# One product of the second input phase as seven inner products, its sums loaded by the next block

## The chip, the cores and the metric

The kernel runs on one core of one Trainium2 chip. The metric is the device time of one execution in microseconds, lower is better; where several runs are shown, their median is meant. TensorE multiplies a stationary operand (loaded by its own instruction) by a moving one into PSUM banks; VectorE (DVE), ScalarE (ACT) and GpSimd (POOL) work elementwise; SyncE (SP) issues most DMAs, POOL some.

## The reference

```python
def pool_mixer(h, in_w, group_w, group_b, scale, out_w):
    b, s, _ = h.shape
    u, gate = jnp.split(h @ in_w, 2, axis=-1)
    ug = u.reshape(b, s, POOL_GROUPS, POOL_GROUP_DIM)
    pooled = jnp.stack([trailing_mean(ug[:, :, g], w) for g, w in enumerate(POOL_WINDOWS)],
                       axis=2) - ug
    mixed = jnp.einsum('bsgc,gcd->bsgd', pooled, group_w) + group_b
    y = mixed.reshape(b, s, POOL_WIDTH) * scale * jax.nn.silu(gate)
    return y @ out_w
...
    h = x
    for i in range(DEPTH):
        normed = rms_norm(h, norm_w[i])
...
            h = h + pool_mixer(normed, pool_in_w[j], pool_group_w[j], pool_group_b[j],
                               pool_scale[j], pool_out_w[j])
    return rms_norm(h, final_norm_w)
```

DEPTH is 1, so there is one such layer: 4096 rows of 1024 channels, float32; the input projection has 2048 columns (1024 pooled over trailing windows of 2, 4, 8 and 16 rows in four groups of 256, and 1024 that become the SiLU gate), the output projection 1024.

## The kernel before

**The products.** The group maps are folded into the input weights at the start, so that three phases of dense products are left: `a` (pooled groups 0 and 1 with their gates), `b` (groups 2 and 3 with theirs, the *second input phase*) and `o` (the output projection). Phases `a` and `b` run over 4 blocks of 1024 rows (TB, NB); a block multiplies 1024 channels by 1024 columns as one step of Strassen's method in Winograd's form: seven products P1 to P7 of 512 x 512 x 512 in place of eight, in the order P1, P2, P7, P6, P5, P4, P3 (ORDER_IN, line 32). The list `steps` (line 1069) holds all of them, and the loop at line 1325 writes them out one by one.

**One product.** Every float32 operand is split into a high and a low half (`split`, line 167: ACT copies the high half rounded to float32r, DVE subtracts it from the source), and a product is made of three passes (high x high, high x low, low x high; `mm3`, line 598). `product_in` (line 609) issues 2 halves x 4 column tiles x 2 x 3 = 48 matmuls with a 128x128 stationary tile of weights and 512 moving rows. The operands of the activations lie in four buffers `op0` to `op3`, two to a product, so that the split for the next product can begin when the product before the current one leaves its buffers.

**The sums.** With the four quarters of the activations (11, 12, 21, 22), `form_in` (line 547) forms S3 = 11 - 21, S2 = 22 - S3 and S1 = S2 + 11, and `form_s4` (line 592) S4 = 12 - S2, each as two tiles of 128x1024. In phase `a` they are formed from x, normalized by row; `split_in` (line 576) stores four of them (P1, P2, P7 and P4's operands) to `sd` in DRAM on POOL's queue. Phase `b` loads these four (`load_saved`, line 528) and forms the other three again, for every block. The weights of phase `b` are formed from T3 (`save_t3`, line 289: the difference of two saved weight tiles, stored to `t3d`) and loaded parts (`load_wb`, `form_wb`, `split_wb`).

**Results.** Banks 0 to 3 take P1, P2, P7 and P4, banks 4 to 7 P6, P5 and P3, on top of a copy of P1 (`bank_of`, line 607). `evict_in` (line 806) takes the rows out: P2 the first gate, P6 and P4 the second, P7 and P5 the rows of one half, P3 those of the other. `pool` (line 745) then does the trailing sums on DVE, multiplies with the gate and stores to `yd` on SP's queue; `pool_later` (line 1116) says how many steps later it is written.

**Order.** Each engine's queue is filled by a scheduler that goes by the order of the program text, by when operands are modelled to be ready, by `issue_after` (not ahead of a given instruction on that engine) and by `high_priority`. SBUF tiles come from two lists of slots, 11 of `st` and 8 of `vt`; `take` picks the one that has been free longest, `give` returns it, and a load into a slot waits for the slot's last user. `keep` takes a slot out for good.

**An inner level** is there already in phase `o`: the product P2 of blocks 2 to 7 is done as seven products of half the size (`split_inner`, `product_inner`, `add_inner`, lines 669 to 711) with matmuls of 256 columns (line 701).

Of the kernel before, what the change touches and what calls it, by code (L numbers as in the profile page):

```python
# [35 lines left out]
class Slots:  # L36
# [4 lines left out]
    def __init__(self, tiles):  # L41
        self.free = deque((0, t) for t in tiles)
        self.used = {}

    def age(self):
# [8 lines left out]
    def keep(self):  # L54

        return self.renew(self.free.popleft()[1])

    def give(self, ap):
# [6 lines left out]
def kernel(  # L65
# [53 lines left out]
    st = Slots(sts)  # L119

    def renew(t):
        i = next(i for i, u in enumerate(sts) if u is t)
        return mem.tile([P, D], F32R, tag=f"st{i}", name=f"inner{i}")

    st.renew = renew
    vt = Slots(
# [40 lines left out]
    def split(dst, src):  # L167
# [17 lines left out]
        for i in range(P1, P7 + 1)  # L185
# [3 lines left out]
            i: [dram.tile([P, 2, H], F32, name=f"sd{b}_{i}_{h}") for h in range(2)]  # L189
            for i in (P1, P2, P7, P4)  # L190
        }
# [85 lines left out]
    def load_wb(i):  # L277
        for h in range(2):
# [5 lines left out]
            for name, place, used in (("t3", t3d[h], (P6, P7)), ("22", wvd[2 + h], (P5, P3))):  # L284
                if i in used:
                    p[name] = take()
                    nc.sync.dma_start(out=p[name], in_=place)

    def save_t3():

        for h in range(2):
            us = []
            for k in (h, 2 + h):
                us.append(take())
                nc.sync.dma_start(out=us[-1], in_=wvd[k])
            with tc.issue_after(evicted[0]):
                sub(us[0], us[1], us[0])
            nc.sync.dma_start(out=t3d[h], in_=us[0])
            for u in us:
                give(u)  # L300

# [21 lines left out]
    def split_wb(i):  # L323
        for h in range(2):
            (u,) = parts.pop((i, h)).values()
            if i == P1:
                split_scaled(w[i][h], u, pair(norm_c, h, 0))
            elif i == P2:
                split_scaled(w[i][h], u, pair(norm_c, h, 1))
            else:  # L330
                split(w[i][h], u)
            if i != P6:
                give(u)
# [165 lines left out]
    xs = [{} for _ in range(NB)]  # L499
    turn = [0]  # L500

    def next_op(pattern, **sizes):
# [33 lines left out]
    def load_in(q, b, i):  # L536
        s = xs[b]
        if i == P1:
            s["11"] = load_saved(b, P1) if q else load_x(b, 0, 0)
        elif i == P2:  # L540
            s["12"] = load_saved(b, P2) if q else load_x(b, 0, 1)
        elif i == P7:
            s["21"] = load_saved(b, P7) if q else load_x(b, 1, 0)
        elif i == P6:
            s["22"] = load_saved(b, P4) if q else load_x(b, 1, 1)

    def form_in(q, b, i):

        s = xs[b]
        if i in (P1, P2):  # L550
            if q == 0:
# [24 lines left out]
    def split_in(q, b, i):  # L576
        s = xs[b]
        key = {P1: "11", P2: "12", P6: "2", P7: "21", P5: "11", P4: "22", P3: "12"}[i]
        later = q == 0 and b == 0 and i in (P1, P2)
        t = split_halves(s[key], None if q or later else sd[b].get(i))  # L580
        if later:
            stores.extend(zip(sd[0][i], s[key]))
        if i == P6 and (q or b):
            form_s4(b)
        if i not in (P1, P2, P7, P6):
            for u in s.pop(key):
                give(u)
        return t
# [18 lines left out]
    bank_of = {P1: "x", P2: "x", P6: "y", P5: "y", P3: "y", P7: "v", P4: "v"}  # L607

    def product_in(i, t, sets, by_bank, between=None, behind=None):
        ps = sets[bank_of[i]]  # L610
        halves = [(h, ct) for h in range(2) for ct in range(4)]
# [133 lines left out]
    def pool(b, q, half, vs, sgs):  # L745
# [4 lines left out]
        for g in range(2):  # L750
# [36 lines left out]
            for j in range(2):  # L787
# [3 lines left out]
                )  # L791
            nc.sync.dma_start(
                out=yd[2 * b + 1 - half][:, 2 * grp : 2 * grp + 2, :], in_=sg
# [9 lines left out]
    def cells(us, lo=0):  # L803
        return [us[c // 2][:, c % 2, lo:] for c in range(4)]

    def evict_in(b, q, i, sets, seeds=4):
# [22 lines left out]
        elif i == P4:  # L829
            for c, u in enumerate(cells(ev["21"])):  # L830
                add(halved(u), plain(ps[c]), halved(u))
            for u in ev["21"]:
                copy(u, u, AF.Silu)
        else:
# [269 lines left out]
    def run(n, between=None, behind=None, seeds=4):  # L1104
# [5 lines left out]
        else:  # L1110
            product_in(i, split_up.pop(n), sets, i == P1, between, behind)
            evict_in(b, 0 if kind == "a" else 1, i, sets, seeds)
# [208 lines left out]
    scales, summed = {}, []  # L1321
    stages = (P6, P5, P4)
    stages = (P6, P5, P4)

    for n in range(2, len(steps)):
# [122 lines left out]
```

## Time and profile before

| | |
|---|---|
| time, median of 3 runs | 910.89 us (910.77 to 911.06) |
| the profiled execution: its time, its span | 911.84 us, 909.7 us |
| granted TensorE clock, mean | 0.997 |
| DMA, mean over the span | 196 GB/s |

A line of the chain of waits gives start and length in us, engine and line; one of a group gives line, engine, operation, output<-input, shapes and count, then busy us, mean ns, and the idle time before with what ended it. PE is TensorE's matmul, PEld its weight load; a matmul's duration in the profile includes its pipeline, so that the distance from one to the next is read from the chain. A row of the windows gives the stretch, its length, then busy us and count by engine, the granted clock, the DMA engines' share and GB/s. A line of the timeline gives start, length, engine, line, operation, output<-input and count, and in brackets the idle time before.

### The profile page before, as it was taken

What the parts mean: (1) busy time and instruction counts of PE and PEld (TensorE: products, weight loads), DVE (VectorE), ACT (ScalarE), POOL (GpSimd) and SP (SyncE); (2) the same over time, 40 slices, a digit from 0 to 9 for tenths busy, and PEclk for the clock granted to TensorE, in tenths of its full rate; (3) what the DMA queues carried; (4) which work ended last, traced back from release to release, by engine and by line L of the source; (5) the groups of instructions that cost most, each with busy time, mean ns of one, the idle gap of its engine ahead of it and who ended that gap; (6) DMA issues with size and microseconds to landing.
All of it is one profiled execution on the core that took longest, in us unless ns stands there. A gap on an engine that the chain in (4) does not pass through costs nothing.

```text
span 909.7 us, 11455 instructions
## 1 busy us (share of the span) xinstructions
PE 900.6 (99%) x4320; PEld 790.1 (87%) x4320; DVE 764.5 (84%) x909; ACT 461.8 (51%) x693; POOL 49.9 (5%) x124
## 2 busy tenths in 40 slices
PE   9999999999999999999999999999999999999997
PEld 7888888888888888888888888888888898888886
DVE  3889995985995997696798699699989878978886
ACT  7869547547446565355445545644424424335334
POOL 0020100100110000000000000000201001001000
PEclk9999999999999999999999999999999999999998
DMA  9977766577675454116616714636385464464332
GB/s 341 401 291 240 276 235 230 189 270 253 217 272 196 156 202 145 47 64 212 255 47 234 275 70 158 235 105 219 137 280 181 149 226 155 146 232 139 116 139 93
DMA packets 66807, 178.08 MB, mean 196 GB/s; under 512 B 6080, under 2 KB 23872, under 8 KB 66752
## 3 DMA queue, kind: packets, MB, share of 16 engines
q1 hardware_dynamic: 60176, 155.83, 48.8%
q0 software_dynamic: 5856, 20.46, 6.1%
q10 hardware_dynamic: 720, 1.06, 0.3%
q8 instruction: 34, 0.56, 0.2%
q14 instruction: 21, 0.17, 0.1%
HBM read 116.50 MB, written 60.83 MB: 195 GB/s over the span
## 4 chain that ended last, share of the span: by engine, by line
PE 91%; DMA 4%; DVE 3%; issue 1%; ACT 0%; SPq 0%; POOL 0%; DVEq 0%; ACTq 0%; POOLq 0%
PE bank L603 88%; PE bank L701 3%; DMA early<-in_wut 2%; DMA st<-in_x 1%; DMA vt<-yd 1%; DVE vt L1033 1%; PE bank L406 1%; DVE op L159 1%; DVE st L159 0%; DVE vt L916 0%; ACT st L943 0%; DVE vt L162 0%; DVE vt L711 0%; SPq L370 0%; DVE st L1033 0%
## 5 line engine op out<-in xcount | busy, mean ns | idle before, releaser
L603 PE MATMUL bank<-op,w 128*128 128x512 f32 x2688 | 580.9, 379 | 0.0
L603 PEld LDWEIGHTS bank<-op,w 128*128 128x128 f32 x2688 | 508.5, 189 | 71.8 <-ACT bank L165 0.4
L603 PE MATMUL bank<-w,op 128*128 128x512 f32 (+1 forms) x1212 | 262.2, 377 | 0.0
L603 PEld LDWEIGHTS bank<-w,op 128*128 128x128 f32 x1212 | 226.3, 189 | 30.7
L165 ACT ACTIVATE op<-st 128x1024 fp32r<-128x1024 f32 x129 | 134.7, 1053 | 142.2 <-PE bank L603 90.5
L159 DVE TENSOR_TENSOR op<-st,op 128x1024 fp32r<-128x1024 f32 x129 | 156.8, 1222 | 51.7 <-ACT op L165 51.3
L156 DVE TENSOR_TENSOR vt<-vt 128x1024 f32<-128x1024 f32 (+6 forms) x72 | 88.2, 1236 | 0.6
L159 DVE TENSOR_TENSOR op<-vt,op 128x1024 fp32r<-128x1024 f32 x43 | 52.5, 1222 | 19.8 <-ACT op L165 19.6
L165 ACT ACTIVATE vt<-bank 128x512 f32<-128x512 f32 x82 | 47.6, 593 | 41.4 <-PE bank L603 40.5
L165 ACT ACTIVATE op<-vt 128x1024 fp32r<-128x1024 f32 x43 | 45.1, 1053 | 39.3 <-PE bank L603 30.2
L159 DVE TENSOR_TENSOR st<-st,st 128x1024 f32<-128x1024 f32 (+1 forms) x43 | 47.0, 1111 | 2.3 <-ACT st L912 1.3
L165 ACT ACTIVATE bank<-bank 128x512 f32<-128x512 f32 x48 | 27.9, 581 | 32.9 <-PE bank L603 32.9
L1033 DVE TENSOR_TENSOR vt<-bank,vt 128x512 f32<-128x512 f32 (+1 forms) x55 | 37.1, 677 | 7.4 <-PE bank L603 7.0
L165 ACT ACTIVATE st<-bank 128x512 f32<-128x512 f32 x48 | 27.8, 593 | 28.7 <-PE bank L603 22.3
L207 POOL TENSOR_SCALAR oms<-oss 128x2 f32<-128x2 f32 x14 | 8.4, 601 | 565.5 <-ACT st L912 460.6
L159 DVE TENSOR_TENSOR w<-st,w 128x1024 fp32r<-128x1024 f32 x25 | 30.2, 1223 | 7.8 <-ACT w L165 7.8
L165 ACT ACTIVATE w<-st 128x1024 fp32r<-128x1024 f32 x25 | 26.0, 1052 | 14.2 <-PE bank L603 9.6
L788 DVE SCALAR_TENSOR_TENSOR st<-vt,colt,st 128x512 f32<-128x512 f32 x46 | 32.7, 752 | 0.1
L1033 DVE TENSOR_TENSOR st<-bank,st 128x512 f32<-128x512 f32 x42 | 28.8, 692 | 3.9 <-PE bank L603 3.7
L783 DVE SCALAR_TENSOR_TENSOR vt<-vt,vt 128x1024 f32<-128x1024 f32 x24 | 29.4, 1227 | 0.3
L916 DVE SCALAR_TENSOR_TENSOR vt<-vt,ors,st 128x1024 f32<-128x1024 f32 x18 | 22.5, 1282 | 7.9 <-POOL ors L225 7.9
L165 ACT ACTIVATE st<-st 128x1024 f32<-128x1024 f32 x16 | 16.9, 1059 | 21.8 <-DVE st L156 21.7
(132 smaller groups left out, 619.0 us busy)
## 6 DMA issues: line engine op xcount, KB each, us to landing
st<-in_x SPq DMA_DIRECT2D x30, 512.0 KB, 5.3
st<-in_xt SPq DMA_DIRECT2D x28, 512.0 KB, 5.6
sd<-st POOLq DMA_DIRECT2D x28, 512.0 KB, 4.6
vt<-in_x SPq DMA_DIRECT2D x27, 512.0 KB, 4.5
st<-sd SPq DMA_DIRECT2D x24, 512.0 KB, 4.2
yd<-st SPq DMA_DIRECT2D x23, 512.0 KB, 2.6
st<-yd SPq DMA_DIRECT2D x20, 512.0 KB, 4.6
out<-vt SPq DMA_DIRECT2D x18, 512.0 KB, 3.6
```

Of the source, the lines that this page charges most:

```text
L156: nc.vector.tensor_tensor(out=dst, in0=a, in1=b, op=ALU.add)
L159: return nc.vector.tensor_tensor(out=dst, in0=a, in1=b, op=ALU.subtract)
L165: return nc.scalar.activation(dst, src, func)
L207: (nc.vector if on_vector and not first else nc.gpsimd).tensor_scalar(out=ms, in0=ss, scalar1=1.0 / D, scalar2=EPS, op0=ALU.mult, op1=ALU.add)
L406: latest[0] = nc.tensor.matmul(ps, a[:, kk, 2 * j + t, :], maps, start=t + m == 0, stop=t == 1 and m == len(pairs) - 1,).ins
L603: latest[0] = nc.tensor.matmul(ps, a, b, start=start and n == 0, stop=stop and n == 2, skip_group_check=True).ins
L701: latest[0] = nc.tensor.matmul(ps, x1, x2, start=i in (P1, P7) and k + n == 0, stop=k == 1 and n == 2, skip_group_check=True,).ins
L783: nc.vector.scalar_tensor_tensor(out=s[:, :, at : at + H], in0=s[:, :, at : at + H], scalar=1.0 / win, in1=v[:, :, HIST:], op0=ALU.mult, o ...
L788: nc.vector.scalar_tensor_tensor(out=sg[:, j], in0=s[:, j, at : at + H], scalar=bias_c[2 * grp + j], in1=sg[:, j], op0=ALU.add, op1=ALU.mult,)
L916: nc.vector.scalar_tensor_tensor(out=us[j], in0=us[j], scalar=rs[:, j : j + 1], in1=fw[0], op0=ALU.mult, op1=ALU.mult,)
L1033: partial["added"] = nc.vector.tensor_tensor(out=dst, in0=src, in1=dst, op=ALU.add).ins
```

## The change

The product P3 of block 0 in phase `b` is done as seven inner products. Its weights B22 (two tiles, kept by `split_wb`) are summed in three stages during P7, P6 and P5 (`form_inner_in`), into four `st` slots that are lent until the product is over. `split_inner_in` forms the four inner sums of its activations, `split_sums` splits them, and `inner_in` issues the products P1, P2, P4, P6, P3, P7, P5, each of two column tiles, with the copies between banks and the adds to the rows. The operands of the next product are split in the middle of it (`then`). Block 1 stores all seven operands in phase `a` and loads all seven in phase `b`, where its splits get priority. The gates of block 0's P4 are activated after P3; its pooling is put one step later and, with P3's, behind the split of the step that it falls in; the stores of block 0's pooled rows in phase `b` go to POOL's queue. T3 is loaded after P1 of block 3 in phase `a` and formed in the step after, where it was formed after P7 of block 2.

```diff
+    def lend(self):
+        t = self.free.popleft()[1]
+        self.lent.append(self.index_of(t))
+        return self.renew(t)
+    def end(self):
+        for i in self.lent:
+            Slots.clock += 1
+            self.free.append((Slots.clock, self.revert(i)))
...
-            for i in (P1, P2, P7, P4)
+            for i in (ORDER_IN if b == 1 else (P1, P2, P7, P4))
...
+    def load_t3():
+        for k in range(4):
+            for_t3.append(take())
+            nc.sync.dma_start(out=for_t3[-1], in_=wvd[k])
+
     def save_t3():
         for h in range(2):
-            us = []
-            for k in (h, 2 + h):
-                us.append(take())
-                nc.sync.dma_start(out=us[-1], in_=wvd[k])
-            with tc.issue_after(evicted[0]):
-                sub(us[0], us[1], us[0])
-            nc.sync.dma_start(out=t3d[h], in_=us[0])
-            for u in us:
-                give(u)
+            with tc.issue_after(latest_split[0]):
+                sub(for_t3[h], for_t3[2 + h], for_t3[h])
+            nc.sync.dma_start(out=t3d[h], in_=for_t3[h])
+        while for_t3:
+            give(for_t3.pop())
...
-            if i != P6:
+            if i == P3:
+                twofold.setdefault("raw", []).append(u)
+            elif i != P6:
                 give(u)
...
     def load_in(q, b, i):
         s = xs[b]
-        if i == P1:
+        if q and b == with_sums:
+            s[i] = load_saved(b, i)
+        elif i == P1:
...
     def form_in(q, b, i):
         s = xs[b]
+        if q and b == with_sums:
+            return
...
+        if q and b == with_sums:
+            key = i
...
-        if i == P6 and (q or b):
+        if q and i == P3 and inner_at(b):
+            t = split_inner_in(t, s[key])
+        if key != i and i == P6 and (q or b):
             form_s4(b)
-        if i not in (P1, P2, P7, P6):
+        if key == i or i not in (P1, P2, P7, P6):
             for u in s.pop(key):
                 give(u)
...
+    def inner_at(b):
+        return b == 0
+
+    def form_inner_in(stage):
+        pattern, sizes = "p (n k c) -> p n k c", dict(n=2, k=2)
+        if stage == 0:
+            us = twofold.pop("raw")
+            (b11, b12), (b21, b22) = (
+                [u[:, :, n * H // 2 : (n + 1) * H // 2] for n in range(2)] for u in us
+            )
+            raw = twofold["sums"] = [take(pattern, **sizes) for _ in range(2)]
+            (t2, t3), (t1, t4) = ([r[:, n] for n in range(2)] for r in raw)
+            sub(t3, b22, b12)
+            add(t2, t3, b11)
+            sub(t1, b22, t2)
+            sub(t4, b21, t2)
+            for u in us:
+                give(u)
+            return
+        r = twofold["sums"][stage - 1]
+        hi, lo = (st.lend().rearrange(pattern, **sizes) for _ in range(2))
+        copy(hi, r)
+        sub(lo, r, hi.bitcast(F32))
+        give(r)
+        for n, i in enumerate(((P6, P7), (P5, P4))[stage - 1]):
+            twofold[i] = [v[:, n] for v in (hi, lo)]
+
+    def split_inner_in(ts, us):
+        (a11, a21), (a12, a22) = ([quarter(u, g) for g in range(2)] for u in us)
+        vs = [take("p (n k s a) -> p n k s a", n=2, k=2, s=2) for _ in range(2)]
+        (s4, s2), (s3, s1) = ([v[:, n] for n in range(2)] for v in vs)
+        sub(s3, a11, a21)
+        sub(s2, a22, s3)
+        sub(s4, a12, s2)
+        add(s1, s2, a11)
+        t = {
+            P1: [quarter(ts[0][:, x], 0) for x in range(2)],
+            P2: [quarter(ts[1][:, x], 0) for x in range(2)],
+            P4: [quarter(ts[1][:, x], 1) for x in range(2)],
+        }
+        t["sums"] = ((vs[0], (P3, P6)), (vs[1], (P7, P5)))
+        return t
+
+    def split_sums(t, n):
+        v, products = t["sums"][n]
+        o = next_op("p (x n k s a) -> p x n k s a", x=2, n=2, k=2, s=2)
+        split(o, v)
+        give(v)
+        for n, i in enumerate(products):
+            t[i] = [o[:, x, n] for x in range(2)]
+
+    def inner_in(t, sets, then):
+        y, (one, six, seven, five) = sets["y"], sets["v"]
+        weights = {
+            i: [w[P3][h][:, x, :, n * H // 2 : (n + 1) * H // 2] for x in range(2)]
+            for i, (h, n) in {P1: (0, 0), P2: (1, 0), P3: (1, 1)}.items()
+        }
+        rows = ev["12"] = [take_v() for _ in range(2)]
+
+        def go(i):
+            place = {P2: (0, 0), P4: (0, 1), P3: (2, 0)}.get(i)
+            spare = {P1: one, P6: six, P7: seven, P5: five}.get(i)
+            b = weights[i] if i in weights else twofold[i]
+            for ct in range(2):
+                bank, g = (y[place[0] + ct], place[1]) if place else (spare, ct)
+                ps = bank.rearrange("p (a s) -> p a s", s=2)[:, g * P : (g + 1) * P]
+                for k in range(2):
+                    lt = [v[:, k, ct * P : (ct + 1) * P] for v in b]
+                    r = [v[:, k].rearrange("p s a -> p a s") for v in t[i]]
+                    for n, (x1, x2) in enumerate(((lt[0], r[0]), (lt[0], r[1]), (lt[1], r[0]))):
+                        latest[0] = nc.tensor.matmul(
+                            ps, x1, x2, start=i in (P1, P7) and ct + k + n == 0,
+                            stop=k == 1 and n == 2, skip_group_check=True,
+                        ).ins
+
+        def to_rows(bank, *places):
+            src = bank.rearrange("p (c a s) -> p c s a", c=2, s=2)
+            for g, n in places:
+                dst = rows[n][:, :, HIST:].rearrange("p c (s a) -> p c s a", s=2)
+                dst = dst[:, :, :, g * P : (g + 1) * P]
+                add(dst, src, dst)
+
+        go(P1)
+        copy(six, one)
+        go(P2)
+        go(P4)
+        go(P6)
+        copied_on = copy(five, six).ins
+        then()
+        go(P3)
+        for c, dst in enumerate(cells(rows, HIST)):
+            with tc.issue_after(copied_on):
+                evicted[0] = copy(halved(dst), plain(y[c])).ins
+        to_rows(one, (0, 0))
+        to_rows(six, (1, 0))
+        go(P7)
+        to_rows(seven, (1, 0), (1, 1))
+        go(P5)
+        to_rows(five, (0, 1), (1, 1))
+        with tc.issue_after(evicted[0]):
+            gates(ev.pop("gates"))
+
     def product_in(i, t, sets, by_bank, between=None, behind=None):
+        if isinstance(t, dict):
+            inner_in(t, sets, behind)
+            return
...
-            nc.sync.dma_start(
+            (nc.gpsimd if q and inner_at(b) else nc.sync).dma_start(
                 out=yd[2 * b + 1 - half][:, 2 * grp : 2 * grp + 2, :], in_=sg
             )
...
-            for u in ev["21"]:
-                copy(u, u, AF.Silu)
+            if q and inner_at(b):
+                ev["gates"] = ev["21"]
+            else:
+                gates(ev["21"])
...
-            with tc.issue_after(evicted[0]) if i == P6 else nullcontext():
+            with ExitStack() as order:
+                if i == P6:
+                    order.enter_context(tc.issue_after(evicted[0]))
+                if kind == "b" and b == 1:
+                    order.enter_context(tc.high_priority())
                 split_up[n] = split_in(kind == "b", b, i)
...
-            wait = int(b == 0) if kind == "a" else 1 if b < NB - 1 else 2
+            wait = int(b == 0) if kind == "a" else 2 if inner_at(b) or b == NB - 1 else 1
...
-        advance("split", n, split_step, split_reach)
+        due = lambda: advance("split", n, split_step, split_reach)
+        inside = kind == "b" and i == P3 and inner_at(b)
+        if inside:
+            for half in range(2):
+                split_sums(split_up[n], half)
+        else:
+            due()
+        if kind == "b" and b == 0 and i in in_stages:
+            with tc.issue_after(latest_split[0]), tc.issue_after(latest_copy[0]):
+                form_inner_in(in_stages.index(i))
...
-        pool_due(n)
+        behind = kind == "b" and b == 1 and i in (P1, P2)
+        with tc.issue_after(latest_split[0]) if behind else nullcontext():
+            pool_due(n)
...
-        run(n)
-        if kind == "a" and b == 2 and i == P7:
+        run(n, behind=due if inside else None)
+        if inside and not inner_at(b + 1):
+            st.end()
+        if kind == "a" and b == 3 and i == P1:
+            load_t3()
+        elif for_t3:
             save_t3()
```

More of the change, by code (lines that the diff above doesn't have):

```diff
@@ L43, in __init__ @@
         self.used = {}
+        self.lent = []
     def age(self):
@@ L119, with index_of, revert @@
     st = Slots(sts)
+    def index_of(t):
+        return next(i for i, u in enumerate(sts) if u is t)
     def renew(t):
-        i = next(i for i, u in enumerate(sts) if u is t)
-        return mem.tile([P, D], F32R, tag=f"st{i}", name=f"inner{i}")
-    st.renew = renew
+        return mem.tile([P, D], F32R, tag=f"st{index_of(t)}", name=f"inner{index_of(t)}")
+    def revert(i):
+        sts[i] = mem.tile([P, D], F32, tag=f"st{i}", name=f"st{i}")
+        return sts[i]
+    st.index_of, st.renew, st.revert = index_of, renew, revert
     vt = Slots(
@@ L287, in load_wb @@
                     nc.sync.dma_start(out=p[name], in_=place)
+    for_t3 = []
+    def load_t3():
+        for k in range(4):
+            for_t3.append(take())
+            nc.sync.dma_start(out=for_t3[-1], in_=wvd[k])
     def save_t3():
         for h in range(2):
-            us = []
-            for k in (h, 2 + h):
-                us.append(take())
-                nc.sync.dma_start(out=us[-1], in_=wvd[k])
-            with tc.issue_after(evicted[0]):
-                sub(us[0], us[1], us[0])
-            nc.sync.dma_start(out=t3d[h], in_=us[0])
-            for u in us:
-                give(u)
+            with tc.issue_after(latest_split[0]):
[3 more added lines that the diff above has]
+            give(for_t3.pop())
     def scaled(u, cs, other, op):
@@ L500 @@
     turn = [0]
+    with_sums = 1
     def next_op(pattern, **sizes):
@@ L607 @@
     bank_of = {P1: "x", P2: "x", P6: "y", P5: "y", P3: "y", P7: "v", P4: "v"}
+    twofold = {}
+    def inner_at(b):
[23 more added lines that the diff above has]
+            twofold[i] = [v[:, n] for v in (hi, lo)]
@@ L804, in cells, with gates @@
         return [us[c // 2][:, c % 2, lo:] for c in range(4)]
+    def gates(us):
+        for u in us:
+            copy(u, u, AF.Silu)
     def evict_in(b, q, i, sets, seeds=4):
@@ L1111, in run @@
             product_in(i, split_up.pop(n), sets, i == P1, between, behind)
-            evict_in(b, 0 if kind == "a" else 1, i, sets, seeds)
+            if not (kind == "b" and i == P3 and inner_at(b)):
+                evict_in(b, 0 if kind == "a" else 1, i, sets, seeds)
     pending = []
@@ L1321 @@
     scales, summed = {}, []
-    stages = (P6, P5, P4)
-    stages = (P6, P5, P4)
+    stages, in_stages = (P6, P5, P4), (P7, P6, P5)
     for n in range(2, len(steps)):
```

## The prediction

> **What bounds the kernel now.** I read the page first, for the busy times; then the chain of work that ended last in order of time; then the two main shapes of matmul; then the windows of the second input phase, one product long each.
>
> ```profile
> span 909.7 us, 11455 instructions
> PE 900.6 (99%) x4320; PEld 790.1 (87%) x4320; DVE 764.5 (84%) x909; ACT 461.8 (51%) x693; POOL 49.9 (5%) x124
> ```
>
> The chain, with start, length, engine and line (L603 is a product's 512-column matmul, L701 the 256-column matmul of the inner products that the output phase has already):
>
> ```profile
> 46.73 0.84 PE bank L472 x8
> 47.57 655.54 PE bank L603 x3036
> 703.11 3.35 PE bank L701 x30
> 706.46 2.59 PE bank L603 x12
> ...
> 780.65 0.81 PE bank L701 x6
> ```
>
> And the same chain asked for the second input phase alone:
>
> ```profile
> 319.79 160.36 PE bank L603 x743
> ```
>
> 160.36 us over 743 matmuls is 215.83 ns each, and 2.59 us over 12 is 215.8. The 3036 in a row take 655.54 us; at 215.83 ns they would take 655.26. So from 47.57 to 703.11 us at most 0.28 us is waiting. **TensorE is the bound and has no holes to give back**: a change gains only what it takes out of TensorE's own stream, and loses what it adds as a hole.
>
> The matmuls of both input phases (2688 in 56 products of 48) run from 33.4 to 614.5 us:
>
> ```profile
> L603 PEld LDWEIGHTS bank<-op,w x2688: 187/189/192, 33.4 to 614.5; 128*128 128x128 f32 x192
> L603 PEld LDWEIGHTS bank<-w,op x1212: 188/189/193, 614.7 to 902.6; 128*128 128x128 f32 x174
> ```
>
> A product is 48 x 215.83 ns = 10.36 us, so the second input phase begins at 614.7 - 28 x 10.36 = 324.6; P3 of its first block, the product that is replaced, stands at 386.8 to 397.1 (call its start T), and P1 of the second block follows. The windows, by product P6, P5, P4 and P3 of the first block, then P1 and P2 of the second, and under them the first and second block whole:
>
> ```profile
> core 0: us, PE busy (x) PEld busy (x) DVE busy (x) ACT busy (x) POOL busy (x), PEclk, DMA share, GB/s
> 355.70:366.06 10.36, 10.36 (x50) 9.09 (x49) 3.37 (x3) 4.90 (x8) 0.00 (x0) 1.00 0.28 94
> 366.06:376.42 10.36, 10.36 (x50) 9.08 (x49) 4.89 (x6) 3.06 (x5) 0.00 (x0) 1.00 0.18 60
> 376.42:386.78 10.36, 10.36 (x50) 9.08 (x49) 10.36 (x12) 3.51 (x5) 0.00 (x0) 1.00 0.00 0
> 386.78:397.14 10.36, 10.36 (x50) 9.08 (x49) 10.26 (x14) 5.33 (x8) 0.00 (x0) 1.00 0.13 51
> 397.14:407.50 10.36, 10.36 (x50) 9.08 (x49) 10.32 (x11) 4.54 (x8) 0.00 (x0) 1.00 0.13 53
> 407.50:417.86 10.36, 10.36 (x50) 9.09 (x49) 10.33 (x11) 3.71 (x7) 0.00 (x0) 1.00 0.54 199
> ```
>
> ```profile
> 324.62:397.14 72.52, 72.52 (x338) 63.57 (x337) 59.90 (x66) 34.68 (x47) 0.00 (x0) 1.00 0.33 115
> 397.14:469.66 72.52, 72.52 (x338) 63.58 (x337) 59.54 (x59) 34.54 (x52) 0.00 (x0) 1.00 0.45 167
> ```
>
> TensorE is full at clock 1.00 in every one. DVE is full around P3 but has 7.0 and 5.5 us free in the windows from 355.70 and 366.06.
>
> **The change, part by part.**
>
> *The matmuls.* Removed: 48 x 215.83 ns = 10.36 us. Added: seven inner products of 2 column tiles x 2 halves of the sum x 3 passes = 84 matmuls of 256 columns, the form of L701: 3.35 us over 30 is 111.7 ns each. 84 x 111.7 = 9.38 us. **Net -0.98 us.** Two rows say how sure that is. The eight 128-column matmuls of L472 take 0.84/8 = 105 ns, hardly less than those of 256 columns, so something other than columns (the weight loads, one per matmul, are what is left) sets the pace just below 111.7 ns: halving again would gain nothing, and the gain here is not larger. The slowest piece of L701, 0.81/6 = 135 ns, is the upper end: 84 x 135 = 11.34 us, +0.98. I take 111.7, the row of the very shape in a long run; the range keeps both.
>
> The Trainium skill speaks against short matmuls here: "TensorE: Matmul & The Clock Gate", section "Back-to-back issue gap", says that a sustained stream of load-and-matmul pairs runs at about 81 ns for 128 columns where the columns alone ask for about 56. Were those 25 ns on top of the 109 that it gives for 256 columns, an estimate from that page is 84 x 134 ns = 11.3 us and a product 0.9 us longer. This trace disagrees for 256 columns (111.7 ns), and its own 128-column row is 105.
>
> *The vector and scalar work of the first block.* Durations:
>
> ```profile
> L165 ACT ACTIVATE op<-st 128x1024 fp32r<-128x1024 f32 x129 | 134.7, 1053 | 142.2 <-PE bank L603 90.5
> L159 DVE TENSOR_TENSOR op<-st,op 128x1024 fp32r<-128x1024 f32 x129 | 156.8, 1222 | 51.7 <-ACT op L165 51.3
> L165 ACT ACTIVATE vt<-bank 128x512 f32<-128x512 f32 x82 | 47.6, 593 | 41.4 <-PE bank L603 40.5
> L165 ACT ACTIVATE bank<-bank 128x512 f32<-128x512 f32 x48 | 27.9, 581 | 32.9 <-PE bank L603 32.9
> ```
>
> ```profile
> L156 DVE TENSOR_TENSOR vt<-bank,vt 128x512 f32<-128x512 f32 x32 | 20.9, 684 | 0.0
> L159 DVE TENSOR_TENSOR vt<-vt,vt 128x512 f32<-128x512 f32 x2 | 1.3, 688 | 0.0
> ```
>
> DVE gets four sums of weights (4 x 0.69 = 2.8), two low halves of them (2 x 1.22 = 2.4), four sums of activations (2.8), two low halves (2.4) and six adds out of the banks (6 x 0.68 = 4.1): +14.5 us. ACT gets four high halves and two bank copies: 4 x 1.05 + 2 x 0.58 = +5.4 us. The second block loses six full-tile sums of DVE (6 x 1.22 = -7.3). Over both blocks DVE goes from 59.90 + 59.54 = 119.4 to 126.6 of 144 us. The weight sums (5.2) fit into the 12.5 free us from 355.70 to 376.42, in front of P3. Against that, the pooling of P4 (14 us in the rows from 375.18 on) is moved behind the split for P2 of the second block, and P3's behind the next one. This empties the windows before T and fills those from 397 to 430, where 10.4 x 3 us must hold 28 of pooling and 7.3 of splits; from 417.86 there are free windows before. Nothing waits for pooled rows but their stores until the output phase. On the path: nothing.
>
> *What must be ready inside the inner P3.* Its seven products of 1.34 us run P1, P2, P4, P6, P3, P7, P5. Before and after T:
>
> ```profile
> 381.99 1.06 ACT L165 ACTIVATE op<-st 128x1024 fp32r<-128x1024 f32 x1 [2.71 <-PE bank L603]
> 387.17 1.06 ACT L165 ACTIVATE op<-vt 128x1024 fp32r<-128x1024 f32 x1 [0.27 <-PE bank L603]
> ```
>
> ```profile
> 375.18 1.24 DVE L156 TENSOR_TENSOR vt<-vt 128x1036 f32<-128x1036 f32 x1
> ...
> 384.53 1.28 DVE L156 TENSOR_TENSOR st<-bank,st 128x512 f32<-128x512 f32 x2
> ...
> 386.86 0.68 DVE L156 TENSOR_TENSOR st<-bank,st 128x512 f32<-128x512 f32 x1
> ...
> 388.72 1.22 DVE L159 TENSOR_TENSOR op<-vt,op 128x1024 fp32r<-128x1024 f32 x1
> ```
>
> P4's two operand buffers come free at 381.99 and 387.17, when today the operands of the next P1 go there. Now the two tiles of sums go there. The first serves inner P6 and P3 from T + 4.02, the second P7 and P5 from T + 6.70; the second is done like today's at 388.72 + 1.22 = 389.94, which is T + 3.1. Bank 0, now inner P1's, is emptied by the first add at 384.53, before T; the last two banks follow by T + 2.0 and are wanted from T + 4.02. Cost nothing, cover 1 us and more.
>
> The operands of the next P1 go into buffers that come free at T + 1.34 and T + 4.02 in place of T - 4.8 and T + 0.4. With 1.06 + 1.22 us the second is done at T + 6.3; the next P1 begins at T + 9.38: cover 3.1 us in place of 7. This is the largest cover that is given up, and it needs ACT at once.
>
> Last the banks: the next P1 overwrites bank 0 at T + 9.38. The copy from the second to the fourth spare bank waits for inner P6 (T + 5.36) and ends at T + 5.94; the row copies follow it (0.59 each), the first two by T + 7.1; the add out of bank 0 ends at T + 7.8. Cover 1.6 us. I cost it at nothing; what it costs with that cover gone is the first rival.
>
> *First phase, second block.* Six more stores of 512 KB on POOL's queue, after which their buffers come free.
>
> ```profile
> L515 POOL DMA_DIRECT2D sd<-st x25: 531/537/554, 53.2 to 269.2; - x25
> ...
> DMA to landing us min/median/max: 2.9/3.8/12.2
> ```
>
> ```profile
> 144.58 2.89 SPq L524 DMA_DIRECT2D st<-in_xt  x2
> ```
>
> ```profile
> 162.92 1.20 DVE L162 TENSOR_TENSOR st<-st,vt 128x1024 f32<-128x1024 f32 x1
> ```
>
> ```profile
> st<-in_xt SPq DMA_DIRECT2D x28, 512.0 KB, 5.6
> ```
>
> The third block's first x tiles are issued by 147.5, land 5.6 later, and are first multiplied at 162.9: 9.8 us of cover against a median landing of 3.8. The row factors of the next block go through the same queue, behind at most two more issues of 0.54 us. Cost nothing.
>
> *Second phase, second block.* Fourteen loads in place of eight.
>
> ```profile
> 356.64 12.95 SPq L532 DMA_DIRECT2D st<-sd  x3
> ```
>
> These are the last of the second block's eight loads, done some 27 us ahead of T + 10; four borrowed buffers make them later, by one or two products at most, and the stores of the first block's pooled rows, which wait for DVE, are taken off SP's queue and put on POOL's, which is idle there (0.00 in the windows). T3 a block later is still formed about two products ahead of its first load. Both cost nothing.
>
> *Sum*: the profiled execution took 911.84 us, 2.14 around a span of 909.7 and 0.95 over the median of the runs shown. 909.70 - 0.98 gives a span of 908.72, a profiled time of 910.86, and a median of 910.89 - 0.98 = **909.9 us**. What a measurement tells from no change here is about 0.2%, 1.8 us: faster means below 909.07, slower above 912.71.
>
> **Rivals.**
>
> *Bank 0 late (the other side).* If ACT does the row copies ahead of the next P1's operands, or DVE has an add of 1.24 us and the operands' halves in front, the chain ends later than T + 9.38: row copies until T + 8.3, operands until T + 10.5, their low halves until 11.7, against T + 9.38 and T + 10.7 (the second half). That is a hole of 1.2, with one DVE instruction ahead 2.5 us: 911.1 to 912.4, say 911.8. It makes the kernel slower than before as soon as the hole is over 0.98. For it: the cover of 1.6 us and a DVE that is full there; against it: ACT is half idle, and the second block's splits get priority.
>
> *Buffers late.* If two store landings at their longest (12.2) stand one behind the other in front of an x load, 24.4 - 9.8 of cover - 10.4 for the product that an operand is ahead = 4.2 us of hole: 914.1. Against it: the median landing of 3.8, and six stores spread over three products.
>
> *Narrow matmuls at 135 ns*: 910.89 + 0.98 = 911.9. Against it: 111.7 over whole runs of 30.
>
> *The inner product doesn't take over* (the old 48 run on): 910.9. The diff leaves no way for that: the dictionary that P3's split returns is what picks the new path.
>
> **How the numbers follow.** Forecast 0.62, bank 0 late 0.16, buffers late 0.12, slow narrow matmuls 0.05, no take-over 0.02, faster by a cause that I don't see 0.03 (only 0.28 us of holes lie in the input phases). The range goes from 909.3, the sum less half a microsecond for those holes and the spread of the runs, to 912.8, which holds the first rival's end of 912.4; it leaves out the buffers and most of the unseen. Slower by over 0.2%: the buffers and a tail of the bank's, 0.17. Faster: 0.03. Same: 0.80.
>
> **What would show it.** L603 falls by 48, the new line's 84 matmuls stand at 111.7 ns, and the chain still shows TensorE alone from 47.57 to 702. A PE idle time ahead of the second block's P1, released by DVE's add out of a bank or by an operand, shows the first rival; a DVE or ACT wait on x near 170 us or on a saved sum near 400, with a hole behind it, the second; the mean of the new line the third. A hole anywhere that names none of these makes the prediction wrong.

## The result and the profile after

The changed kernel takes 919.25 us in the median of 6 runs (915.57 to 919.73), the kernel before 910.87 (910.66 to 911.06): a ratio of 1.0085, 95% interval 1.0069 to 1.0101. It is slower by 8.4 us, where 909.9 was forecast and 912.8 was the end of the range. The profiled execution took 919.71 us with a span of 917.9.

The page's first lines, of the changed kernel:

```profile
span 917.9 us, 11578 instructions
PE 904.1 (98%) x4356; PEld 792.4 (86%) x4356; DVE 770.8 (84%) x921; ACT 467.1 (51%) x699; POOL 54.2 (6%) x134
```

TensorE now has pauses. The chain that ended last, in order of time (L635 is the 512-column matmul, L719 the new inner products, L846 the output phase's inner ones):

```profile
47.15 339.56 PE bank L635 x1572
386.71 9.39 PE bank L719 x84
...
440.45 153.29 PE bank L635 x695
...
669.05 20.57 PE bank L635 x94
...
720.48 0.94 PE bank L846 x6
```

The 84 new matmuls take 9.39 us, 111.8 ns each, and nothing waits inside the product: that term came out as forecast. The 695 matmuls after 440.45 should take 150.0 us at 215.83 ns and take 153.29. TensorE's own waits, which the timeline gives in brackets, show the first pause, of 2.92 us:

```profile
440.45 5.06 PE L635 MATMUL bank<-op,w 128*128 128x512 f32 x11 [2.92 <-ACT st L183]
```

Windows of that pause and of what follows it (columns as before: stretch, length, busy us and count of PE, PEld, DVE, ACT and POOL, granted clock, DMA share, GB/s):

```profile
437.54:440.45 2.91, 0.00 (x0) 0.00 (x0) 0.00 (x0) 1.25 (x3) 0.00 (x0) 0.88 1.02 386
440.45:446.70 6.25, 6.25 (x15) 4.98 (x16) 5.59 (x5) 2.97 (x5) 0.00 (x0) 0.51 0.91 347
```

TensorE runs at half clock for 6.25 us behind the pause: 15 matmuls where 29 fit, which makes 3.0 of the other 3.3 us (153.29 - 150.0). By TensorE's timeline the two profiles add up: from the products that begin at 46.99 to the output phase's first inner product at 710.16 it is 663.2 us, where it was 655.5 (47.41 to 702.95). That is +7.6, and -0.97 (inner product) + 2.92 (pause at 437.5) + 3.29 (half clock) + 2.15 (pause at 666.9, in the output phase) = +7.4. What follows adds 1.0 more, 0.76 of it a pause at 719.7; the start was 0.4 us earlier. In sum +8.2, which is the difference of the spans.

What TensorE waited for at 437.5 is read along the chain of waits, from 396 to 442:

```profile
424.60 6.31 DMA yd<-vt
...
430.93 0.34 SPq L556
...
431.91 7.26 DMA st<-in_out_w
439.17 0.02 issue
439.20 0.03 ACT st L264
...
439.82 0.59 ACT st L183
440.41 0.04 issue
440.45 1.65 PE bank L635 x3
```

and in ACT's timeline at the same place:

```profile
433.70 1.33 ACT L264 ACTIVATE st<-st,colt 128x512 f32<-128x512 f32 x2 [3.23 <-DMA st<-in_out_w]
434.94 1.04 ACT L183 ACTIVATE op<-st 128x1024 fp32r<-128x1024 f32 x1
439.20 0.72 ACT L264 ACTIVATE st<-st,colt 128x512 f32<-128x512 f32 x1 [3.21 <-DMA st<-in_out_w]
439.82 0.58 ACT L183 ACTIVATE st<-bank 128x512 f32<-128x512 f32 x1
```

A store of pooled rows of the first block goes out on POOL's queue at 424.60 and lands at 430.91. Only then may SP load a saved operand into its tile (L556, 430.93). Behind that load in SP's queue stands a part of the output weights (issued at 431.91, landed 7.26 us later). ACT has the scaling of these weights (L264) at the head of its queue and waits 3.21 us for them, while the copies that empty P6's banks (L183 from `bank`) stand behind it. P5 of the second block writes these banks next, and TensorE waits. In the kernel before, the scaling (L246 there) stood ahead of the same copies (L165 from `bank`) too, but the last part of the weights was issued by 426.1, the scaling was through at 434.4, and the first copy followed at 435.26:

```profile
432.47 1.94 ACT L246 ACTIVATE st<-st,colt 128x512 f32<-128x512 f32 x3
434.31 1.04 ACT L165 ACTIVATE op<-st 128x1024 fp32r<-128x1024 f32 x1
435.26 0.58 ACT L165 ACTIVATE st<-bank 128x512 f32<-128x512 f32 x1
```

Nothing in this chain was on the forecast's list of waits, although each link is a tile, a queue or a line that the kernel had already.

DVE shows why the rows of that store are late. From 396.10 to 437.50, first in the kernel before, then in the changed one:

```profile
396.10:437.50 41.40, 41.40 (x194) 36.30 (x193) 32.02 (x31) 22.66 (x35) 0.00 (x0) 1.00 0.45 162
```

```profile
396.10:437.50 41.40, 41.40 (x192) 35.93 (x191) 38.70 (x43) 20.52 (x32) 2.15 (x4) 1.00 0.57 192
```

DVE goes from 32.0 to 38.7 us in these 41.4: the pooling that was put behind the next splits.

### The profile page after: what moved, and what is told of

The parts are those of the page before. It is cut to its first block, busy times and chain, and to the rows that moved or that the text cites. A ratio compares the mean times of both kernels' runs of the same rounds, so it can differ in the third digit from the quotient of the medians.

```text
span 917.9 us, 11578 instructions
## 1 busy us (share of the span) xinstructions
PE 904.1 (98%) x4356; PEld 792.4 (86%) x4356; DVE 770.8 (84%) x921; ACT 467.1 (51%) x699; POOL 54.2 (6%) x134
## 4 chain that ended last, share of the span: by engine, by line
PE 79%; DVE 11%; DMA 4%; issue 4%; ACT 1%; POOL 0%; SPq 0%; DVEq 0%; ACTq 0%; POOLq 0%
PE bank L635 74%; PE bank L846 3%; DVE vt L174 3%; DVE op L177 2%; DMA early<-in_wut 1%; PE bank L719 1%; DMA st<-in_x 1%; PE bank L429 1%; DMA st<-in_out_w 1%; DVE st L1184 1%; DVE st L177 1%; DMA yd<-vt 1%; DVE w L177 1%; DVE st L1067 1%; DVE st L174 1%
## 5 line engine op out<-in xcount | busy, mean ns | idle before, releaser
L635 PE MATMUL bank<-op,w 128*128 128x512 f32 x2640 | 574.0, 381 | 2.9 <-ACT st L183 2.9
L635 PEld LDWEIGHTS bank<-op,w 128*128 128x128 f32 x2640 | 500.8, 190 | 75.2 <-ACT st L183 3.3
L635 PE MATMUL bank<-w,op 128*128 128x512 f32 (+1 forms) x1212 | 262.5, 377 | 2.2 <-DVE op L177 2.2
L635 PEld LDWEIGHTS bank<-w,op 128*128 128x128 f32 x1212 | 226.0, 189 | 33.5 <-DVE op L177 2.6
L183 ACT ACTIVATE op<-st 128x1024 fp32r<-128x1024 f32 x134 | 140.3, 1053 | 142.6 <-PE bank L635 92.3
L177 DVE TENSOR_TENSOR op<-st,op 128x1024 fp32r<-128x1024 f32 x134 | 162.5, 1220 | 48.1 <-ACT op L183 47.5
L174 DVE TENSOR_TENSOR vt<-vt 128x1028 f32<-128x1028 f32 (+6 forms) x72 | 87.9, 1231 | 0.6
L183 ACT ACTIVATE vt<-bank 128x512 f32<-128x512 f32 x94 | 54.3, 594 | 36.1 <-PE bank L635 35.9
L183 ACT ACTIVATE op<-vt 128x1024 fp32r<-128x1024 f32 x40 | 41.9, 1054 | 48.3 <-PE bank L635 31.6
L177 DVE TENSOR_TENSOR op<-vt,op 128x1024 fp32r<-128x1024 f32 x40 | 48.6, 1219 | 13.1 <-ACT op L183 12.9
L177 DVE TENSOR_TENSOR st<-st,st 128x1024 f32<-128x1024 f32 (+1 forms) x39 | 42.1, 1096 | 8.2 <-ACT st L264 6.7
L183 ACT ACTIVATE bank<-bank 128x512 f32<-128x512 f32 x50 | 29.0, 581 | 36.9 <-PE bank L635 36.6
L1184 DVE TENSOR_TENSOR vt<-bank,vt 128x512 f32<-128x512 f32 (+1 forms) x53 | 35.5, 675 | 7.3 <-PE bank L635 7.0
L177 DVE TENSOR_TENSOR w<-st,w 128x1024 fp32r<-128x1024 f32 x26 | 31.4, 1219 | 7.8 <-ACT w L183 7.8
L183 ACT ACTIVATE w<-st 128x1024 fp32r<-128x1024 f32 x26 | 27.0, 1052 | 17.1 <-PE bank L635 12.0
L183 ACT ACTIVATE st<-bank 128x512 f32<-128x512 f32 x36 | 21.0, 593 | 25.6 <-PE bank L635 17.1
L174 DVE TENSOR_TENSOR vt<-bank,vt 128x512 f32<-128x512 f32 (+1 forms) x49 | 31.8, 678 | 2.6 <-PE bank L635 2.0
L928 DVE SCALAR_TENSOR_TENSOR vt<-vt,vt 128x1024 f32<-128x1024 f32 x24 | 29.2, 1221 | 0.3
L1067 DVE SCALAR_TENSOR_TENSOR vt<-vt,ors,st 128x1024 f32<-128x1024 f32 x17 | 21.2, 1282 | 8.6 <-POOL ors L243 8.6
L180 DVE TENSOR_TENSOR st<-st,vt 128x1024 f32<-128x1024 f32 x22 | 26.1, 1216 | 1.8 <-DMA vt<-rd 1.8
```

What stands on the lines that cost most here:

```text
L174: nc.vector.tensor_tensor(out=dst, in0=a, in1=b, op=ALU.add)
L177: return nc.vector.tensor_tensor(out=dst, in0=a, in1=b, op=ALU.subtract)
L180: nc.vector.tensor_tensor(out=dst, in0=a, in1=b, op=ALU.mult)
L183: return nc.scalar.activation(dst, src, func)
L635: latest[0] = nc.tensor.matmul(ps, a, b, start=start and n == 0, stop=stop and n == 2, skip_group_check=True).ins
L928: nc.vector.scalar_tensor_tensor(out=s[:, :, at : at + H], in0=s[:, :, at : at + H], scalar=1.0 / win, in1=v[:, :, HIST:], op0=ALU.mult, o ...
```

## The experiments

All times are medians; the kernel before ran beside each group (910.98 beside e1 to e4, 911.07 beside e5 to e8, 911.18 beside e9 and e10, 911.35 beside e11). Ratios are to it, with 95% intervals. Pauses are read from the one profiled execution of each kernel.

| run | edit | us | ratio |
|---|---|---|---|
| e1 | changed kernel, scaling behind P6's bank copies | 913.43 | 1.0027 [1.0017, 1.0036] |
| e2 | changed kernel, pooling and gates at their old step | 915.64 | 1.0047 [1.0032, 1.0062] |
| e3 | changed kernel, second block forms its sums | 917.05 | 1.0062 [1.0045, 1.0079] |
| e4 | kernel before, T3 one block later | 910.88 | 0.9996 [0.9987, 1.0006] |
| e5 | e1 and priority for one split of the output phase | 911.95 | 1.0006 [0.9997, 1.0015] |
| e6 | e2 with e1's edge | 912.96 | 1.0020 [1.0011, 1.0029] |
| e7 | kernel before with e5's priority | 911.28 | 1.0002 [0.9993, 1.0011] |
| e8 | kernel before with e1's edge | 911.18 | 1.0002 [0.9993, 1.0011] |
| e9 | e6, adds out of the spare banks first | 910.35 | 0.9989 [0.9980, 0.9997] |
| e10 | e9, second block forms its sums | 910.73 | 0.9993 [0.9984, 1.0002] |
| e11 | changed kernel, pooled rows stored from SP | 915.67 | 1.0045 [1.0030, 1.0061] |

**e1: is it the order in ACT's queue?**

```diff
-                scale_rows(us[kh, n], pair(scale_c, h, kh))
+                with tc.issue_after(evicted[0]):
+                    scale_rows(us[kh, n], pair(scale_c, h, kh))
```

> The changed kernel with one edge more: ACT's scaling of the output weights is queued behind the copies that empty P6's banks. Theory (the first hole is ACT's queue: a scaling that waits for a late load stands ahead of P6's bank copies): the hole of 2.9 us near 437 and the half clock after it (3.3 us) go, 913 us. Rival (DVE's backlog itself makes operands late): the hole stays in another place, 917 to 920 us. If all that is left is also caused by the delay, 910 us.

913.43 us. The chain of this run from 370 to 440 has TensorE and nothing else:

```profile
369.84 16.62 PE bank L636 x77
386.46 9.38 PE bank L720 x84
395.83 44.25 PE bank L636 x205
```

Its store is no earlier (424.36 on POOL) and its weights no earlier either (the last part issued at 433.22). Only the order on ACT differs: the scaling runs in one piece from 438.80, behind the bank copies. So a load as late as this costs nothing by itself; a wait at the head of ACT's queue costs 2.9 us and, with the clock, 6. What stays in e1 are the pauses of the output phase, 2.15 and 0.76 us.

**e2: is late pooling the source?**

```diff
-            if q and inner_at(b):
-                ev["gates"] = ev["21"]
-            else:
-                gates(ev["21"])
+            gates(ev["21"])
...
-        with tc.issue_after(evicted[0]):
-            gates(ev.pop("gates"))
...
-            wait = int(b == 0) if kind == "a" else 2 if inner_at(b) or b == NB - 1 else 1
+            wait = int(b == 0) if kind == "a" else 2 if b == NB - 1 else 1
...
-        behind = kind == "b" and b == 1 and i in (P1, P2)
+        behind = False
```

> The changed kernel with the first block's gates and pooling put back to their old step and not behind the next splits. Theory (late pooling holds the gate's tile, whose store then holds SP's queue): no load stands behind a store near 431, the hole near 437 is gone, about 913 us; the inner product loses its cover on DVE by at most 1.2 to 2.5 us. Rival (the six more loads alone fill the queue): the hole stays, 918 to 920 us.

915.64 us, which neither side had, and the theory as I had put it falls: with pooling early, three pauses stand in the second input phase, of 1.20 us at 397 (released by DVE's add out of bank 0), 1.00 at 401, and 2.51 at 440. Here a part of the output weights waits for another store of pooled rows, which is on POOL's queue as in the changed kernel:

```profile
420.36 8.70 DMA yd<-st
429.06 0.02 issue
429.08 4.19 DMA st<-in_out_w
...
438.37 3.22 DMA st<-in_out_w
441.59 0.02 issue
441.61 0.05 ACT st L264
...
442.24 0.58 ACT st L183
```

Late pooling is thus not needed for a late load. Both kernels have the stores on POOL's queue, the borrowed slots and the six more loads, and in both ACT's queue turns the delay into a pause. e11 tests the first of these; what the borrowed slots and the loads add by making tiles scarce was not run alone. The two pauses at 397 and 401 are what the later pooling had kept away, and they are the first rival of the prediction.

**e3: is it the loaded sums?**

```diff
-    with_sums = 1
+    with_sums = None
...
-            for i in (ORDER_IN if b == 1 else (P1, P2, P7, P4))
+            for i in (P1, P2, P7, P4)
```

> The changed kernel, but the second block loads four operands and forms three, as before. Theory (late pooling): the SP queue still meets a slot that a pooled row holds, so a hole of 1 us or more stays near 420 to 440, 914 to 919 us. Rival (the six more loads and stores make the hole): no hole there, 912 to 914 us.

917.05 us: a pause again, but in another place and by another wait. TensorE's timeline there has 4.26 us before 420.73, and the chain leads to it through DVE, which still pools when a tile of P2's gate is wanted:

```profile
416.57 1.15 DVE vt L174
417.72 1.14 DVE st L177
418.86 1.15 DVE vt L928
420.00 0.02 issue
420.02 0.02 ACTq L183
420.04 0.04 issue
420.08 0.61 ACT vt L183
420.69 0.04 issue
420.73 4.63 PE bank L635 x10
```

ACT's copy of P2 out of the banks waits for a tile that the pooling step before it (L928) still uses. Forming the sums (`st` L177 in these lines) stands between the pooling steps and makes this wait longer. Even so this run is 2.2 us faster than the changed kernel: its output phase has one pause of 0.34 us in place of 2.15 and 0.76. So nothing here shows that the loaded sums pay with late pooling, and they are no condition of a pause near 420 to 440.

**e4: T3 alone.** The two functions and their calls as in the change, put into the kernel before.

> The kernel before with T3 alone formed one block later. Both theories: no hole, 910.9 us within 0.3. If the later T3 changes the order in which slots go round so that the output phase stalls, 912 to 914 us with a hole near 660.

910.88 beside 910.98: no effect, as forecast. **e7 and e8** (the edges of e5 and e1 put into the kernel before) are controls:

> The kernel before with e5's priority alone. Theory: that kernel has no hole near 660, so nothing changes, 911.0 within 0.5. Rival (the priority is a gain by itself): 910 or less.

> The kernel before with e1's edge alone. Theory: its loads are early enough, nothing to gain, 911.0 within 0.5. Rival (the edge is a gain by itself): 910 or less.

Both came out within 0.25 us of the kernel before. The edges are no gain by themselves; they mend what the change broke.

**e5: the pause in the output phase.** In DVE's queue of the changed kernel both pairs of the final scaling of the first rows (L1067, at 659.64 and 665.38) stand ahead of the low half of P6's operand of the next block (667.78), and so they do in e1. In the kernel before, that operand (658.74) stands between the two pairs (656.27 and 660.86).

```diff
-            split_up[n] = split_o(b, i)
+            with tc.high_priority() if b == 1 and i == P6 else nullcontext():
+                split_up[n] = split_o(b, i)
```

> e1 and, in the output phase, priority for the split of block 1's P6, so that its operand stands ahead of the final scaling in DVE's queue. Theory (the hole of 2.15 us near 660 is an order in DVE's queue and nothing is short): it goes, and 913.4 falls to about 911; with the 0.76 us hole near 714 gone too, 910.0. Rival (the output phase lacks time because the second block's work was pushed into it): the hole moves to another place, 912.5 to 914.

911.95 us: the pause near 660 is gone, but one of 1.13 us (released by an operand) stands at 702.7 and the one of 0.76 at 712.4. So the order there was the cause of that pause, and another pause comes without it. This lies between the theory (910.0 to 911) and the rival (912.5 to 914). The changed order stands only in the changed kernel, e1 and e11, which have late pooling and loaded sums together; e3 (sums formed), e2, e6 and e9 (pooling early) have the order of the kernel before. In e6 and e9 TensorE's timeline marks no pause in the output phase, so the loaded sums leave it time enough in that order. Why the scheduler writes the other one, and where the pause of 0.76 us comes from, I did not settle.

**e6: both sides of the trade.** e2 with e1's edge.

> e2 with e1's edge: pooling early, scaling behind P6's bank copies. Theory: the hole of 2.5 us near 441 goes and those of 1.20 and 1.00 us near 397 and 401 stay (bank 0 emptied late, since early pooling stands in DVE's queue there): 915.6 falls to 912.5 to 913.2. Rival (bank 0's holes were an accident of that order): 910.5 or less.

912.96 us, as forecast, and the two pauses of the first block alone are left:

```profile
397.26 2.86 PE L636 MATMUL bank<-op,w 128*128 128x512 f32 x12 [1.20 <-DVE vt L174]
401.11 3.07 PE L636 MATMUL bank<-op,w 128*128 128x512 f32 x13 [1.00 <-ACT bank L183]
```

**e9: a version without pauses.** DVE gets the adds out of the first three spare banks by priority:

```diff
-        to_rows(one, (0, 0))
-        to_rows(six, (1, 0))
+        with tc.high_priority():
+            to_rows(one, (0, 0))
+            to_rows(six, (1, 0))
         go(P7)
-        to_rows(seven, (1, 0), (1, 1))
+        with tc.high_priority():
+            to_rows(seven, (1, 0), (1, 1))
```

> e6 with priority for the adds out of the inner product's first three spare banks. Theory (the first block's two holes are only the order in DVE's queue): both go and nothing is left but the shorter product, 912.96 - 2.2 = 910.8 or less, down to 910.1. Rival (the adds displace the operands of the next products): holes of 1 us or more near 397 to 410, 912 or more.

910.35 beside 911.18 us: faster than the kernel before, by an interval that excludes 1 but by less than the 1.8 us that the prediction asked of a difference. The adds out of banks 0 and 1 are now done by 395.9, 1.3 us earlier than the first of them in e6. The chain shows TensorE alone from 47.38 to 510.5, and TensorE's timeline marks no pause from there to the end of the output phase:

```profile
47.38 339.56 PE bank L636 x1572
386.94 9.62 PE bank L720 x84
396.56 113.97 PE bank L636 x528
```

The difference of -0.83 us is about the shorter product (-0.98) and the wait inside it, which makes it 9.62 us in place of 9.39.

**e10: e9 without the loaded sums.**

> e9 with the second block loading four operands and forming three, as before. If the loaded sums are what keeps DVE's backlog short, a hole near 420 as in e3, 912 to 915; if pooling early is enough, the same as e9, 910.1 to 910.8.

910.73 us, no pause near 420. With pooling at its old step the loaded sums are not needed; whether they gain anything is not settled, since the two intervals overlap.

**e11: the store's queue alone.**

```diff
-            (nc.gpsimd if q and inner_at(b) else nc.sync).dma_start(
+            nc.sync.dma_start(
```

> The changed kernel with the first block's pooled rows stored from SP's queue, as before, and nothing else undone. If the store's long landing on POOL's queue (6.3 us, where SP's take 2.6 to 3.2) is what makes the load late, the hole near 437 shrinks below 1 us, 913 to 916 us. If the rows are late because DVE forms them late, the loads stand behind the stores in SP's own queue and the hole near 437 stays at 2 us or more, 917 us or more.

915.67 us. The pause near 437 shrinks to 0.48 us. The two stores that went out on POOL at 424.60 and 425.70 go out on SP from 423.47 on, and between 420 and 440 they land after 5.1 us in the median, where POOL's two took 6.8. The last part of the weights is asked for at 430.95 in place of 431.91, and ACT's last wait for weights ahead of the bank copies ends at 436.24 in place of 439.20. That the stores were moved to POOL thus cost most of the pause, though they were moved in order to keep SP's queue free. The pauses of the output phase stay (2.15 and 0.76), and in this run it is the one of 2.15 that brings the half clock.

## Why the prediction was wrong

**The product itself** was forecast at 9.38 us and took 9.39; the 134 and 135 ns that were set against it did not come, with 111.8 ns each for 256 columns.

**T3** costs nothing in the kernel before (e4), as forecast.

**The step that failed** is one oversight in two terms that were put at nothing. On the moved pooling the prediction says: "Nothing waits for pooled rows but their stores until the output phase. On the path: nothing." On the stores it says that they "are taken off SP's queue and put on POOL's, which is idle there", at no cost. Both ask who reads the pooled rows and not who needs the tiles that they lie in. The tile goes back to a load in SP's queue, and that queue holds the output weights, whose scaling stands in ACT's queue ahead of a bank copy. The sum lacked this term, which measured 2.92 us of pause and 3.29 us of half clock in the profile; the one edge of e1 took out 5.8 us. That DVE would fall behind stood in the prediction's own numbers, 28 us of pooling and 7.3 of splits in 31.2 us.

The companion step, that four borrowed buffers make the second block's loads later "by one or two products at most", looked at the saved operands, which had 27 us of cover, and not at the weights behind them. In the kernel before, the eight loads were out by 369.6; in the changed kernel SP still issues loads of saved operands until 409.2, and the four parts of the output weights go out from 421.54 to 431.91, where they went out from 418.53 to 425.77.

**The stores on POOL** were taken as relief, since that queue is idle. e11 shows the opposite: with the pooling as late and the stores on SP, 0.48 of the 2.92 us are left. In e2, with the pooling early and the stores on POOL, 2.51 us stand. By these two runs the queue of the stores is the larger of the two terms. Early pooling with the stores on SP was not run.

**The output phase** was not in the sum at all. Its pauses of 2.15 and 0.76 us in the changed kernel stay in e1. e5 shows that the order of two DVE instructions made the first; how an edit of the input phase came to change that order stays open, and so does the second.

**The rivals.** Bank 0's rival was right as a mechanism: its pauses of 1.20 and 1.00 us appear as soon as pooling is early (e2, e6), inside the 1.2 to 2.5 us that were given. In the changed kernel the later pooling keeps them away, which I had entered as free of cost and not as what it was for. The rival "buffers late" (914.1, 0.12) named the right kind of cause and put it ahead of the x loads of the first phase, where nothing happened. That the cover of 1.6 us on bank 0 was enough in the changed kernel is luck: it held because of the later pooling and not by the reason given. By the prediction's own last sign, a pause that names none of its rivals, it is wrong twice, at 437 and at 667.

## What to carry to other kernels

When work is moved later, list the tiles that it holds and follow each tile to the next load, then everything behind that load in its queue, and on to the engine that waits for it: here it was a transfer behind the blocked one that cost. An instruction whose load can come late should not stand ahead of a bank copy on the same engine: one ordering edge was worth 5.8 us in the changed kernel, and nothing in the kernel before, whose load was early (e8). With TensorE full at 99%, a saving of 1 us is only there if the order of every engine around it stays as good as it was, so the profile after is to be read for pauses in all phases, also far from the edit.

## What the hardware showed

The granted clock falls to half behind pauses that are shorter than I would have thought, and not each time. Two windows of e11, the pause of 2.15 us and what follows:

```profile
661.75:663.90 2.15, 0.00 (x1) 0.01 (x1) 2.15 (x3) 0.44 (x1) 0.00 (x0) 1.00 0.73 292
663.90:667.60 3.70, 3.70 (x9) 2.98 (x10) 3.70 (x5) 0.00 (x0) 0.00 (x0) 0.54 0.81 288
```

and the same pause in e1:

```profile
660.45:662.60 2.15, 0.00 (x1) 0.01 (x1) 2.15 (x3) 0.44 (x1) 0.00 (x0) 1.00 0.74 294
662.60:666.30 3.70, 3.70 (x17) 3.27 (x18) 3.70 (x5) 0.00 (x0) 0.00 (x0) 1.00 0.79 284
```

The same length gives 9 matmuls in 3.70 us in the one and 17 in the other; e2's pause of 2.51 us left the clock at 1.00, that of 2.92 in the changed kernel did not. The Trainium skill, "TensorE: Matmul & The Clock Gate", section "HAM oscillation — how this bites in real kernels", asks for no gaps on TensorE above some 3.4 us. These runs differ on the length: 2.15 us can be enough. The section "What's actually happening" on that page of the Trainium skill says that the window in which the clock gate watches TensorE is free-running and does not start with the kernel. That would fit one length of pause with and without the half clock, but no run here shows the window itself.

The half clock would also explain part of why the changed kernel's runs spread over 4.2 us (915.57 to 919.73) where those before it lie within 0.4, since a pause with and without it differs by 3.3. The fastest run has a mean granted clock of 0.999 and the other five 0.994 to 0.997, which agrees; which pause brought it in each run was not shown.
